# A WKV kernel on one Trainium2 core: a new hand-written order of all steps, with the first 21 loads on SyncE

## The chip, the cores and the metric

The kernel runs on one core of one Trainium2 chip. The metric is the device time of one execution in microseconds (us). A core has five engines that each work through a queue of their own, in order: TensorE (PE, with its weight loads PEld), VectorE (DVE), ScalarE (ACT), GpSimd (POOL) and SyncE (SP), which here only issues transfers. An instruction that has to wait holds up all that stands behind it in the queue of its engine. That holds for transfers too, since they are issued by instructions of POOL and SP.

## The reference

```python
# k, v: [16, 2048, 256] float32; w, u: [256]
for b in range(batch):
    aa, bb, pp = 0, 0, -1e38                      # per channel
    for t in range(seq_len):
        qq = maximum(pp, u + k[b, t])
        e1, e2 = exp(pp - qq), exp(u + k[b, t] - qq)
        output[b, t] = (e1 * aa + e2 * v[b, t]) / (e1 * bb + e2 + 1e-08)
        qq = maximum(pp - w + k[b, t], k[b, t])
        e1, e2 = exp(pp - w + k[b, t] - qq), exp(k[b, t] - qq)
        aa, bb, pp = e1 * aa + e2 * v[b, t], e1 * bb + e2, qq
```

It is a recurrence over time, apart for each batch and channel: a weighted mean of v, whose numerator `aa` and denominator `bb` are carried on with a running maximum `pp`.

## The kernel before, in words

The time axis is cut into 16 chunks of 128 steps, the 16 batches into four groups of four. A chunk of one group is a piece, n = 4 * chunk + group, so there are 64 pieces. A piece of k, of v and of the output is 512 KB each (`rows_of`, lines 126 to 128). The steps of a piece, by the short names that the order uses:

- `sk`, `k` load k, issued by SP or by POOL, into one of NK tiles `kr` (line 228). `sv`, `v` load v into one of NV tiles `vr` (line 238), and `CV` casts it on POOL to bf16 in one of NVB tiles `vb` (line 244). `vc` loads v with the cast in the transfer, into one of NVC tiles `vc` (line 241), and needs no `CV`; only POOL issues it. A load into a tile waits until the former piece in that tile has been read.
- `RK` rounds k on DVE into one of two tiles `km` (line 231).
- `LG` and `LGZ` make the logarithms of all weights on PE (lines 254 and 260). Pieces before H and from S on have two banks of half a piece each: `x` and `y` for even pieces, `d` and `n` for odd pieces before H. Between H and S there is one tile `X` of four banks in the place of `x` and `y`, and `d` and `n` are left to the sums below.
- `EXE` and `EX` take the exponential on ACT into the ring `ez` of 11 pieces: in halves (line 288, 1024 columns each), or in one instruction over `X` (line 286, 2048 columns).
- `TV` multiplies by v on DVE into the ring `ev` of 11 pieces (line 292).
- `DE` and `NU` make denominator and numerator on PE in 12 small matmuls each (line 306): sums over earlier steps, the step itself, and the row `RW` carried in from the chunks before.
- `LN` and `XP` turn the denominator into its inverse on ACT (lines 318 and 321) in one of NO output tiles `ot`, `MU` multiplies by the numerator on DVE (line 324), and `ST` stores with three transfers on SP (lines 328 and 330).

From the sums of a chunk's four pieces a chain of small steps makes the carry that the next pieces need, across four engines: `SU` (PE, line 360, reads `ez` and `ev` of four pieces), `CS` (DVE, 367), `TU` (PE, 372), `CT` (DVE, 377), `SL` (ACT, 380), `SH` (POOL, 385), `FR` (DVE, 390), `OF`, `OF2`, `OF3` (POOL, 395, 397, 399), `WE` (ACT, 402), `TBM`, `SCN`, `SPR` (DVE, 405, 410, 414), `TB` (PE, 426) and `RW` (DVE, 430). `KP` (POOL, 420 and 421) keeps the totals for the next chunk. `DE` and `NU` of chunk c wait for `RW` of c. Since `ez` holds 11 pieces, the exponentials of piece n wait for `DE` of piece n - 11 and for the `SU` that reads it.

`Z` and `Y` are matmuls with zeros (line 187) into a bank that is written over afterwards: they compute nothing and keep PE busy.

All of this stands in one list, `ORDER`, which is read from front to back; each word issues its instructions on their engines, so the list fixes the order in every queue. A letter d, n, x or y behind a word names the bank. Ahead of the list the program issues the loads of w and u on POOL, the first piece of k on SP, 13 zero matmuls (LEAD), and the constants, which POOL makes.

Of the kernel before, what the change touches and what calls it, by code (L numbers as in the profile page):

```python
# [21 lines left out]
H = 10  # L22
# [465 lines left out]
```

## Time and profile before

| | us |
|---|---|
| three runs | 290.6, 292.18, 294.44 |
| median | 292.18 |
| the profiled execution: its time | 294.63 |
| the profiled execution: its span, first to last instruction | 292.9 |
| busy in the span: PE, ACT, DVE, POOL | 253.2, 249.7, 244.7, 181.9 |

The profiled execution is 2.45 us above the median, and 1.73 us of its time lie outside its span. Times in the trace are counted from the start of the span. The profile page gives busy shares in 40 slices, groups of like instructions with the mean of one in ns, and the idle time ahead of them with what ended it. An answer by windows gives busy time for each engine in stretches that the reader chooses; the timeline gives single instructions in order, with their start, their duration and, in brackets, the idle time before them and what ended it. GB/s count a cast load by the bytes that it writes, half of those that it reads.

### The profile page before, as it was taken

The page shows a single profiled execution, that of the slowest core. Times are in us where ns is not written, and L with a number is a line of the kernel's source. Part 1 is how long each engine was busy: PE and PEld are TensorE (multiplying, and loading weights), DVE is VectorE, ACT ScalarE, POOL GpSimd, SP SyncE. Part 2 cuts the span into 40 slices and gives each one's busy share as a digit, 9 for nine tenths or more (in the row PEclk, how much of TensorE's full clock was granted, in tenths as well). Part 3 has the DMA queues.
Part 4 walks back from the last instruction along what each step waited for, and adds up shares of the span by engine and source line. Part 5 has one row for each costly group of instructions (what it writes and reads, how often), then busy time and mean ns, then how long its engine had stood idle before and what let it go on. Part 6 is the DMA issues. An engine that isn't in the chain of part 4 may idle for free. (4 is left out here: it accounts for less than half of the span.)

```text
span 292.9 us, 7115 instructions
## 1 busy us (share of the span) xinstructions
PE 253.2 (86%) x2775; PEld 132.8 (45%) x2775; DVE 244.7 (84%) x337; ACT 249.7 (85%) x243; POOL 181.9 (62%) x274
## 2 busy tenths in 40 slices
PE   8997988989889969989899999987988899898920
PEld 3444444545445434554445454544454455444410
DVE  4456669889889869999999999899999889898760
ACT  1774648989998888999999999999899999999960
POOL 7558968586777874668676958476657746432000
PEclk9998979999999999999999999999999999999995
DMA  7999997999999999999999999999999999995797
GB/s 227 348 348 329 358 189 247 329 385 286 373 346 294 383 359 398 357 313 289 373 352 344 403 288 352 391 313 296 386 333 309 352 317 364 310 273 158 226 265 215
DMA packets 70913, 93.54 MB, mean 319 GB/s; under 512 B 5204, under 2 KB 60000, under 8 KB 70880
## 3 DMA queue, kind: packets, MB, share of 16 engines
q0 software_dynamic: 27648, 52.19, 59.2%
q1 hardware_dynamic: 43232, 40.91, 45.4%
q8 instruction: 21, 0.34, 0.5%
q14 instruction: 12, 0.10, 0.1%
HBM read 67.12 MB, written 33.55 MB: 344 GB/s over the span
## 5 line engine op out<-in xcount | busy, mean ns | idle before, releaser
L286 ACT ACTIVATE ez<-X 128x2048 bf16<-128x2048 f32 x46 | 86.4, 1878 | 9.0 <-PE X L260 8.8
L324 DVE TENSOR_TENSOR ot<-n,ot 128x1024 f32<-128x1024 f32 x59 | 71.8, 1217 | 7.6 <-PE n L306 2.2
L321 ACT ACTIVATE ot<-ot 128x1024 f32<-128x1024 f32 x64 | 67.5, 1060 | 0.2
L318 ACT ACTIVATE ot<-d 128x1024 f32<-128x1024 f32 x58 | 59.6, 1027 | 2.4 <-PE d L306 1.9
L231 DVE CAST km<-kr 128x1024 fp32r<-128x1024 f32 x64 | 47.2, 743 | 11.5 <-DMA kr<-in_k_dram 9.4
L228 POOL DMA_DIRECT2D kr<-in_k_dram x56 | 44.2, 790 | 14.5 <-DVE km L231 9.4
L244 POOL CAST vb<-vr 128x1024 bf16<-128x1024 f32 x35 | 40.8, 1168 | 16.3 <-DMA vr<-in_v_dram 16.1
L292 DVE TENSOR_TENSOR ev<-ez,vb 128x2048 bf16<-128x2048 bf16 x35 | 45.0, 1288 | 2.7 <-POOL vb L244 2.7
L292 DVE TENSOR_TENSOR ev<-ez,vc 128x2048 bf16<-128x2048 bf16 x29 | 37.4, 1291 | 0.6 <-ACT ez L288 0.4
L260 PE MATMUL X<-km,NLE 128*128 128x512 f32 x92 | 33.7, 447 | 0.8 <-DVE km L231 0.8
L306 PE MATMUL n<-ev,LN 64*64 64x512 bf16 x236 | 24.0, 391 | 8.3 <-DVE ot L324 3.2
L254 PE MATMUL X<-WU,CO 1*128 1x512 f32 (+1 forms) x184 | 23.3, 495 | 6.4 <-ACT ez L286 5.6
L260 PE MATMUL X<-km,NLZ 128*128 128x512 f32 x92 | 28.8, 394 | 0.0
L306 PE MATMUL d<-ez,L 64*64 64x512 bf16 x232 | 23.7, 392 | 2.8 <-DVE RW L430 1.9
L238 POOL DMA_DIRECT2D vr<-in_v_dram x29 | 23.9, 823 | 2.5 <-DMA vc<-in_v_dram 1.5
L241 POOL DMA_DIRECT2D vc<-in_v_dram x29 | 23.2, 801 | 2.1 <-DVE TB L405 1.4
L306 PE MATMUL n<-RW,ROW 64*64 64x512 bf16 x236 | 23.5, 376 | 0.0
L306 PE MATMUL n<-ev,IdN 64*64 64x512 bf16 x236 | 23.5, 376 | 0.0
L306 PE MATMUL d<-RW,ROW 64*64 64x512 bf16 x232 | 23.2, 380 | 0.0
L306 PE MATMUL d<-ez,Id 64*64 64x512 bf16 x232 | 23.2, 380 | 0.0
L385 POOL TENSOR_TENSOR U<-U 128x64 f32<-128x64 f32 x16 | 9.5, 592 | 21.3 <-ACT U L380 21.2
L288 ACT ACTIVATE ez<-x 128x1024 bf16<-128x1024 f32 x13 | 13.3, 1025 | 10.7 <-PE x L254 5.4
(97 smaller groups left out, 431.6 us busy)
## 6 DMA issues: line engine op xcount, KB each, us to landing
kr<-in_k_dram POOLq DMA_DIRECT2D x56, 512.0 KB, 9.7
out_dram<-ot SPq DMA_DIRECT2D x64, 256.0 KB, 10.2
out_dram<-ot SPq DMA_DIRECT2D x128, 128.0 KB, 10.0
vr<-in_v_dram POOLq DMA_DIRECT2D x29, 512.0 KB, 9.6
vc<-in_v_dram POOLq DMA_DIRECT2D x29, 256.0 KB, 10.5
kr<-in_k_dram SPq DMA_DIRECT2D x8, 512.0 KB, 8.0
vr<-in_v_dram SPq DMA_DIRECT2D x6, 512.0 KB, 7.8
WU<-in_w_dram POOLq DMA_DIRECT2D x1, 8.0 KB, 5.3
```

Of the source, the lines that this page charges most:

```text
L228: K(q.dma_start(out=buf[n % len(buf)], in_=rows_of(x, n)))
L231: K(DVE.tensor_copy(KM[n % 2], KR[n % NK]))
L238: K(q.dma_start(out=VR[V_TILE[n] % NV], in_=rows_of(v, n)))
L244: K(POOL.tensor_copy(VB[V_TILE[n] % NVB], VR[V_TILE[n] % NV]))
L254: K(PE.matmul(log_tile(n, q)[:, i, :], CO[g:g + 1 + q, :], WU[g:g + 1 + q, :], start=q > 0 or n != FIRST, stop=q == 0 and n == FIRST, tile ...
L260: K(PE.matmul(log_tile(n, q)[:, i, :], (NLE, NLZ)[q], km[:, i, :], start=q == 0 and n == FIRST, stop=q > 0 or n != FIRST, skip_group_check ...
L286: K(SC.activation(t, BANKS["X"], ACT.Exp))
L292: K(DVE.tensor_mul(EV[n % REV], EZ[n % RING], vb.unsqueeze(1).broadcast_to([128, 2, 2, D])))
L306: K(PE.matmul(t[HS * x:HS * x + HS, i, :], left, right, start=j == 0, stop=m == "ROW", tile_position=(lo, HS * x), skip_group_check=True))
L318: K(SC.activation(OT[n % NO], AT.pop(("den", n)), ACT.Ln, scale=RS))
L321: K(SC.activation(OT[n % NO], OT[n % NO], ACT.Exp, scale=-1.0))
L324: K(DVE.tensor_mul(OT[n % NO], AT.pop(("num", n)), OT[n % NO]))
```

## The change

Seven loads go from POOL to SP: SP issues k.0 to k.12 and v.0 to v.7, 21 loads, where it issued k.0 to k.7 and v.0 to v.5. `v.7`, which was a load with cast, becomes a plain load with a `CV`; there are 28 loads with cast where there were 29. NK goes from 7 to 6 and NVC from 4 to 6 (a k tile has 4 KB in a partition, a `vc` tile 2 KB). H goes from 10 to 8: pieces 8 and 9 use the tile `X`. All other steps are the same in kind and number, but stand in a new order, and some of `SU`, `TU`, `TB`, `DE` and `NU` use another bank. There are 43 `Z` where there were 46, and 55 `Y` where there were 28. No function is changed.

The places that the prediction speaks of (the head of the list, its part behind the last exponential, and the words around it in between):

```diff
-NK = 7
+NK = 6
 NV = 3
-NVC = 4
+NVC = 6
...
-H = 10
+H = 8
...
 ORDER = """
-    sk.1 sv.0 sv.1 sk.2 sk.3 sv.2 sk.5 sk.4 RK.0 LG.0 RK.1 Z.1 Z.1 Z.1 Z.1 EXE.0 CV.0 LGZ.0 CV.1 LG.1 sv.3 EX.0 RK.2
-    sv.4 TV.0 Z.2 Z.2 Z.2 EXE.1 LGZ.1 LG.2 RK.3 EX.1 CV.2 LGZ.2 EXE.2 Z.3 Z.3 Z.3 Z.3 TV.1 sv.5 EX.2 LG.3 sk.6 sk.7
-    LGZ.3 EXE.3 RK.4 Z.4 Z.4 Z.4 Z.4 Z.4 Z.4 RK.5 EX.3 TV.2 LG.4 CV.3 Z.5 Z.5 EXE.4 LGZ.4 k.9 LG.5 TV.3 EX.4 k.8
-    LGZ.5 EXE.5 CV.4 Z.6 Z.6 Z.6 Z.6 Z.6 Z.6 EX.5 v.6 TV.4 vc.7 SU.0d RK.6 LG.6 CS.0 k.10 CV.5 TU.0d EXE.6 LGZ.6
-    CT.0 v.8 Z.7 Z.7 Z.7 Z.7 Z.7 Z.7 SL.0 EX.6 SH.0 RK.7 k.11 FR.0 LG.7 TV.5 k.12 Z.8 Z.8 Z.8 EXE.7 OF.0 RK.8 LGZ.7
-    OF2.0 LG.8 EX.7 RK.9 OF3.0 CV.6 Z.9 Z.9 EXE.8 LGZ.8 LG.9 TV.7 v.10 WE.0 EX.8 k.13 TBM.0 EXE.9 Z.10 Z.10 SCN.0
-    LGZ.9 vc.9 RK.10 EX.9 TV.6 LG.10 vc.11 vc.15 SPR.0 TB.0d EX.10 CV.8 SU.1n RW.0 KP.0 DE.0d CS.1 RK.11 TU.1n Z.11
-    Z.11 CV.10 CT.1 LG.11 SL.1 LN.0 RK.12 k.18 TV.10 NU.0n v.12 EX.11 DE.1d k.14 TV.9 LN.1 SH.1 Z.12 Z.12 k.15 TV.8
...
-    TV.61 Z.63 LG.63 WE.14 XP.52 MU.51 CV.62 LGZ.63 DE.53d EXE.63 TV.62 ST.51 NU.52n LN.53 MU.52 EX.63 Y.54 DE.54d
...
+    sk.1 sv.0 sv.1 sk.2 sk.3 sv.2 RK.0 Z.1 Z.1 Z.1 Z.1 Z.1 Z.1 RK.1 LG.0 LG.1 EXE.0 CV.0 LGZ.0 CV.1 sv.3 LGZ.1 EX.0
+    sk.4 RK.2 sk.6 EXE.1 Z.2 Z.2 Z.2 Z.2 sv.4 TV.0 sk.5 LG.2 EX.1 sk.8 RK.3 sk.7 TV.1 LGZ.2 EXE.2 Z.3 Z.3 Z.3 Z.3
+    Z.3 Z.3 EX.2 CV.2 LG.3 CV.3 sv.5 sk.9 LGZ.3 EXE.3 TV.2 Z.4 Z.4 Z.4 Z.4 Z.4 Z.4 EX.3 RK.4 LG.4 sk.10 TV.3 sv.6
+    EXE.4 CV.4 SU.0n LGZ.4 CS.0 EX.4 TU.0n CT.0 RK.5 Z.5 Z.5 Z.5 Z.5 SL.0 SH.0 sk.11 RK.6 LG.5 sv.7 FR.0 sk.12 OF.0
+    Z.6 EXE.5 LGZ.5 OF2.0 LG.6 RK.7 EX.5 CV.5 LGZ.6 EXE.6 Z.7 Z.7 OF3.0 RK.8 vc.9 LG.7 WE.0 EX.6 TBM.0 TV.4 LGZ.7
+    vc.11 EXE.7 Z.8 LG.8 SCN.0 EX.7 SPR.0 KP.0 EX.8 TB.0n CV.6 Y.0 Y.0 Y.0 RW.0 RK.9 v.10 DE.0d TV.5 LG.9 v.8 LN.0
+    k.13 RK.10 NU.0n TV.6 EX.9 k.14 Y.1 DE.1d CV.7 LN.1 LG.10 vc.13 TV.7 XP.0 k.15 RK.11 SU.1d EX.10 CS.1 TU.1d XP.1
+    LG.11 CV.10 RK.12 CT.1 MU.0 Y.2 Y.2 SL.1 EX.11 SH.1 v.12 FR.1 NU.1n ST.0 OF.1 DE.2d OF2.1 MU.1 OF3.1 LG.12 CV.8
+    WE.1 LN.2 ST.1 TV.10 k.16 Y.3 Y.3 Y.3 Y.3 Y.3 EX.12 v.14 TBM.1 RK.13 DE.3d SCN.1 XP.2 k.19 LG.13 TV.11 vc.15
...
+    NU.52n FR.14 LGZ.63 EXE.63 TV.61 Y.53 Y.53 Y.53 DE.53d EX.63 MU.52 OF.14 OF2.14 LN.53 OF3.14 DE.55x TV.63 ST.52
...
```

108 lines of the change are left out of this document (54 added, 54 removed).

## The prediction

> **What bounds the kernel now.** I read the page first: which engines are full, and when.
>
> ```profile
> span 292.9 us, 7115 instructions
> PE 253.2 (86%) x2775; PEld 132.8 (45%) x2775; DVE 244.7 (84%) x337; ACT 249.7 (85%) x243; POOL 181.9 (62%) x274
> ...
> ACT  1774648989998888999999999999899999999960
> ...
> DMA  7999997999999999999999999999999999995797
> ...
> HBM read 67.12 MB, written 33.55 MB: 344 GB/s over the span
> ```
>
> ACT, DVE and PE share the middle, all over nine tenths, with the DMA engines busy beside them. What is not full is the ramp (slices 1 to 8 of ACT) and the end. So I asked for windows over the ramp and the middle (the columns are busy us of PE, PEld, DVE, ACT and POOL, then granted clock, DMA share and GB/s).
>
> ```profile
> 24.00:32.00 8.00, 6.19 (x24) 3.17 (x24) 5.23 (x8) 2.84 (x4) 6.85 (x11) 0.79 1.10 335
> 32.00:38.00 6.00, 5.24 (x27) 2.42 (x25) 4.80 (x6) 5.60 (x7) 6.00 (x8) 1.00 1.03 346
> 38.00:50.00 12.00, 10.37 (x108) 5.21 (x108) 9.20 (x12) 6.97 (x7) 9.09 (x12) 0.86 0.91 188
> ...
> 85.00:113.00 28.00, 23.70 (x277) 12.48 (x270) 24.00 (x34) 23.61 (x22) 19.55 (x26) 1.00 1.13 349
> 113.00:229.00 116.00, 106.32 (x1245) 56.82 (x1245) 110.92 (x146) 111.91 (x103) 80.88 (x115) 1.00 1.11 343
> ```
>
> From 113 on ACT is busy 111.91 of 116. Before that two things show: ACT stands still for 5 of 12 us between 38 and 50, and there the transfers fall from 346 to 188 GB/s. The timelines of ACT, DVE, POOL and PE, one fence each, say why.
>
> ```profile
> 34.70 0.36 ACT L402 ACTIVATE G<-U 128x192 f32<-128x192 f32 x1
> 39.63 1.88 ACT L286 ACTIVATE ez<-X 128x2048 bf16<-128x2048 f32 x1 [1.51 <-PE X L260]
> 44.67 0.34 ACT L380 ACTIVATE U<-TS 128x128 f32<-128x128 f32 x1 [3.16 <-DVE TS L377]
> 46.29 1.88 ACT L286 ACTIVATE ez<-X 128x2048 bf16<-128x2048 f32 x1 [0.36 <-PE X L260]
> 51.89 1.87 ACT L286 ACTIVATE ez<-X 128x2048 bf16<-128x2048 f32 x1
> 55.49 1.88 ACT L286 ACTIVATE ez<-X 128x2048 bf16<-128x2048 f32 x1 [0.31 <-PE X L260]
> 113.12 1.88 ACT L286 ACTIVATE ez<-X 128x2048 bf16<-128x2048 f32 x1 [0.52 <-PE X L260]
> 227.87 1.88 ACT L286 ACTIVATE ez<-X 128x2048 bf16<-128x2048 f32 x1
> ```
>
> ```profile
> 6.41 0.70 DVE L231 CAST km<-kr 128x1024 fp32r<-128x1024 f32 x1 [0.34 <-DMA kr<-in_k_dram]
> 11.12 0.69 DVE L231 CAST km<-kr 128x1024 fp32r<-128x1024 f32 x1 [4.01 <-DMA kr<-in_k_dram]
> 17.14 1.30 DVE L231 CAST km<-kr 128x1024 fp32r<-128x1024 f32 x2 [2.46 <-DMA kr<-in_k_dram]
> 25.68 0.41 DVE L367 COPY ts<-d 128x256 f32<-128x256 f32 x1
> 40.84 0.69 DVE L430 CAST RW<-d 128x512 bf16<-128x512 f32 x1 [1.04 <-PE d L426]
> ```
>
> ```profile
> 31.24 0.44 POOL L399 TENSOR_SCALAR U<-U 128x64 f32<-128x64 f32 x1
> 43.61 0.76 POOL L228 DMA_DIRECT2D kr<-in_k_dram  x1 [2.89 <-DVE km L231]
> ```
>
> ```profile
> 42.09 0.64 PE L306 MATMUL d<-ez,L 64*64 64x512 bf16 x4
> ```
>
> The eight ACT rows are `WE.0`, the exponentials of piece 10, `SL.1`, and pieces 11, 12, 13, 26 and 55. `RW.0` comes at 40.84, so `DE.0` at 42.09. Piece 11 reuses the `ez` tile of piece 0 and must wait for it: 6.66 us lie between pieces 10 and 11. In the same time POOL stands at `k.18`, whose tile is free only after `RK.11` (43.61), with v.12, k.14 and k.15 queued behind it: that is the hole in the transfers. From piece 13 to 26 a piece takes 57.63 / 13 = 4.43 us, from 26 to 55 it takes 114.75 / 29 = 3.96 us. So the bound is a late first carry in the ramp, a stretch that runs behind, then a full ACT (with DVE close to it).
>
> **The change, part by part.** (1) Loads on SP. The three DVE waits above are for the 2nd, 5th and 9th load of SP: 6.41, 11.12, 17.14, or 1.5 us a load. I take load number i (from 0) to land at 5.1 + 1.5 i. In the new row k.4 is still the 9th (17.1), k.6 comes at 18.6, v.4 20.1, k.5 21.6, k.8 23.1, k.7 24.6, v.5 26.1, k.9 27.6, v.6 30.6, v.7 33.6, k.12 35.1. The k come earlier, v.6 and v.7 later. SP issues in order and now waits at `sv.3` for `CV.0`, with thirteen loads behind it, `sk.4` first. `CV.0` and `CV.1` run here:
>
> ```profile
> 8.86 2.02 POOL L244 CAST vb<-vr 128x1024 bf16<-128x1024 f32 x2
> ...
> 14.14 1.45 POOL L244 CAST vb<-vr 128x1024 bf16<-128x1024 f32 x1 [3.25 <-DMA vr<-in_v_dram]
> ```
>
> so SP goes on at about 9.9, while loads already issued land until 14.1 (the second row, for v.2): no hole, 0 us. POOL gives up seven issues and takes one more cast:
>
> ```profile
> L228 POOL DMA_DIRECT2D kr<-in_k_dram x56 | 44.2, 790 | 14.5 <-DVE km L231 9.4 <-DVE TB L405 2.6 <-DVE U L390 1.9
> L244 POOL CAST vb<-vr 128x1024 bf16<-128x1024 f32 x35 | 40.8, 1168 | 16.3 <-DMA vr<-in_v_dram 16.1
> ```
>
> 7 x 0.79 - 1.17 = 4.4 us less, all of it ahead of 36 us, where POOL was full (6.00 of 6.00) and the first carry passed through it.
>
> (2) The first carry. Each step is put after the last one it waits for, with durations from the rows. `TV.3` needs `CV.3` (v.3 at 15.6) and `EX.3`, which slips to some 17.7 behind six zero matmuls, and `RK.4`: it ends at 19.9. `SU.0` 20.0 to 21.2; `CS.0` 21.2 (it was 25.68, queued behind `RK.6`, whose k.6 was the 13th load); `SL.0` 22.9; `SH.0`, `FR.0` (behind `RK.5` and `RK.6`) until 24.5; `OF.0`, `OF2.0` until 25.6; then POOL has `CV.5` ahead of `OF3.0` and waits for v.5: 26.1 + 1.17, `OF3.0` ends at 27.7 (it was 31.68); `WE.0` 27.8 (34.70); `SCN.0` behind `TV.4` 29.6; `TB.0` behind `LG.8` 31.3; `RW.0` 31.7 (40.84); `DE.0` 32.5 (42.09). The carry comes 9 us earlier.
>
> (3) Pieces 8 to 13, with H = 8. A piece over `X` needs 1.9 us on PE and then 1.88 on ACT, one after the other. The LN and XP that the early carry sets free fill ACT meanwhile. `EX.8` 31.5, `EX.9` 35.5, `EX.10` 39.2 (it was 39.63); `EX.11` waits for nothing of the ring now, only for PE behind `TU.1`: 43.3 (46.29); `EX.12` 47.0 (51.89); `EX.13` 50.8 (55.49). That is 4.7 us. `LN.3` is done by then, which it was not before: one more instruction off the rest.
>
> ```profile
> L318 ACT ACTIVATE ot<-d 128x1024 f32<-128x1024 f32 x58 | 59.6, 1027 | 2.4 <-PE d L306 1.9 <-DMA out_dram<-ot 0.2
> L187 PE MATMUL d<-Z 128*128 128x512 bf16 x46 | 14.5, 409 | 0.5 <-ACT ot L318 0.5
> L286 ACT ACTIVATE ez<-X 128x2048 bf16<-128x2048 f32 x46 | 86.4, 1878 | 9.0 <-PE X L260 8.8
> ```
>
> 1.0 us, so -5.7 in all. Bounds: 0, if a late v.10 eats it (rival C), and 9, the whole advance of the carry.
>
> (4) Pieces 13 to 26. The pace was 4.43 against 3.96 later. If the new order has no hole behind it, up to 13 x 0.47 = 6.1 us more go. If the transfers are as late as before, nothing. I take 0, nearer to the trace: loads on POOL are again queued behind casts and behind tiles not yet free (`CV.10`, `k.19`).
>
> (5) Zero matmuls. 24 more, at most 24 x 14.5 / 46 = 7.6 us of PE. PE is idle for 40 us of the span and they stand ahead of waits: 0. Where that cover is gone (six ahead of `LG.3` and of `LG.4`) they are counted in (2). Bounds -1 (less of the low clock, 0.79 and 0.86 above) and +2.
>
> (6) Two pieces more over `X`: 1.88 for two of 1.02, which is -0.2 each on ACT; but its idle ahead of such a piece is 9.0 / 46 = 0.2. Sum 0. Six tiles for k and other banks for the small sums: 0, bounds below (rival D).
>
> (7) The end.
>
> ```profile
> 282.99 1.23 DVE L324 TENSOR_TENSOR ot<-y,ot 128x1024 f32<-128x1024 f32 x1 [0.79 <-DMA out_dram<-ot]
> ```
>
> ```profile
> 286.31 0.54 SPq L328 DMA_DIRECT2D out_dram<-ot  x1
> ...
> 288.24 0.55 SPq L328 DMA_DIRECT2D out_dram<-ot  x1
> 288.84 1.26 SPq L330 DMA_DIRECT2D out_dram<-ot  x2
> ```
>
> SP issues one store each 1.93 us and is behind the last `MU` by three of them. Twelve stores stand behind the last exponential in both lists, so this stays; one more LN stands there in the new list (`LN.53`): +0.9. Bounds -1 and +2.
>
> Sum: -5.7 + 0 + 0 + 0 + 0.9 = -4.8. The profiled execution (294.63, which is 292.9 and 1.73 around it) would become 289.8. It lies 2.45 above the median of the runs, 292.18; from that, 287.4.
>
> **The rivals.** A is the sum: 287.4, or 284 to 291 by its bounds in (5), (6) and (7) and half of those in (3).
>
> B, the stretch goes too: no hole at 38 to 50, so pieces 13 to 26 run at 3.96. 287.4 - 6.1 = 281.3. For it: in the later stretch 29 pieces of 1.57 MB (k, v and output, 512 KB each) took 114.75 us, 397 GB/s, so the transfers can follow. Against it: 85 to 113 showed 349 GB/s at a share of 1.13 without keeping up, so B gets half the chance of A. The Trainium skill (DMA: Bandwidth & Descriptors, Specifications) gives about 358 GB/s of HBM for a core; by that figure 100.67 MB take an estimated 281 us without ramp or end, and B could not be. The trace's 397 GB/s over 114.75 us do not agree with it.
>
> C, the hole only moves: POOL has `CV.10` ahead of `SH.1`, `v.12` and `OF.1`, and v.10 is issued only after `CV.6`, at about 33. I took it to land in 6.5 us. The view of line 238 gives this for loads into `vr`:
>
> ```profile
> DMA to landing us min/median/max: 5.9/9.5/14.5
> ```
>
> At 14.5 it lands at 47.5, `CV.10` ends near 48.7, and `SH.1` is 7 us late. `RW.1`, which I place at 52, comes at 59 and `DE.4` at 60, when `EX.15`, due near 58.5 (50.8 and two pieces), stands waiting for the `ez` tile: 1.5 us. What was issued before (eight loads on POOL behind 35.1, at 1.5 each) has landed by 47, so the transfers stand for some 3 us until `v.12` and those behind it flow. 287.4 + 4.5 = 291.9. By this the change does not do what it says: the work moves and the time stays.
>
> D, slower: six k tiles starve `RK`. Two rows bear on it, the casts of k and the landing of k's loads.
>
> ```profile
> L231 DVE CAST km<-kr 128x1024 fp32r<-128x1024 f32 x64 | 47.2, 743 | 11.5 <-DMA kr<-in_k_dram 9.4 <-PE n L260 2.1
> ```
>
> ```profile
> kr<-in_k_dram POOLq DMA_DIRECT2D x56, 512.0 KB, 9.7
> ```
>
> With seven a tile can be away for 7 x 3.96 = 27.7 us, with six for 23.8. Of that landing takes 9.7 us in the median, and waits of POOL for a free tile come on top (9.4 us in all, line 228 above). If the pace of 4.43 then lasts to piece 55, it costs 29 x 0.47 = 13.6: 301.0. It decides once more than ten pieces behind the 26th run at that pace (10 x 0.47 = 4.7), and is slower by 2% after 23. Against it: with seven tiles DVE waited 9.4 us for k in all, and 6.8 of them are the three waits before 18.
>
> **How the numbers follow.** Chances: A 0.45, B 0.22, C 0.20, D 0.13. The time is that of A, 287.4. A measurement of this kernel can tell about 2% from no change, so the bounds are 286.3 and 298.0. Below 286.3 lie B and about a third of A: 0.22 + 0.15 = 0.37. Above 298.0 lies most of D: 0.10. Between them: 0.53. The range leaves out the lower half of B and the upper part of D: 280.0 to 296.0; A's own is 284 to 291.
>
> **What the changed profile would show.** Right: `RW.0` (line 430, first) near 32 and the first `DE` near 32.5; no stretch under 300 GB/s between 15 and 60; the fifth exponential over `X`, counting piece 8 as the first, starting at 47, the sixth at 51; POOL's first wait for a free k tile under 1 us. (4) is read from the spacing of line 286 up to its 19th instance (piece 26): 4.43 for A, 3.96 for B. C shows as a wait of POOL for a `vr` load of over 5 us ahead of line 385's second instance. D shows as DVE waits for `kr` all through 113 to 229. The forecast is wrong if `WE.0` still stands after 33, or if the pace behind piece 26 is over 4.1.

## The result and the profile after

The changed kernel is not faster: over 20 runs each, its median is 294.03 us (292.99 to 296.68) against 293.08 (290.6 to 299.75) for the kernel before, a ratio of 1.0054 with a 95% interval of 1.003 to 1.0079. The forecast was 4.8 us less; what came is about 1 us more by the medians and 1.6 by the ratio. The profiled execution took 293.75 us, with a span of 292.0. Every ratio here is made of the undisturbed runs alone, so it need not be the quotient of two medians, and of the four kernels whose profiles were taken in disturbed executions (`e5_ramp_of3`, `e7_old_sp`, `e8_new_to_30`, `e9_old_to_30`) only the timed runs are used.

First the page of the changed kernel: totals, and the slices of ACT, of the granted clock and of the transfers.

```profile
span 292.0 us, 7159 instructions
PE 259.7 (89%) x2799; PEld 133.3 (46%) x2799; DVE 243.6 (83%) x337; ACT 250.6 (86%) x241; POOL 171.4 (59%) x268
...
ACT  1754688978899999989999999999979999999970
...
PEclk9999599999999999999999999999999999999995
DMA  7999998999999999999999999999999999974887
GB/s 224 348 348 351 299 332 246 321 365 329 274 364 341 396 312 345 301 388 400 384 297 399 369 257 392 345 345 393 295 371 319 345 399 307 307 225 111 255 237 214
...
L232 DVE CAST km<-kr 128x1024 fp32r<-128x1024 f32 x64 | 49.9, 784 | 6.5 <-DMA kr<-in_k_dram 6.0
```

Little moved in the totals. ACT has 250.6 us of work where it had 249.7, and PE 259.7 where it had 253.2, part of which is matmuls at a low clock: the fifth slice of PEclk is a 5. In the slices of ACT the sixth, 36.5 to 43.8 us, is an 8 where it was a 4; but the ninth to eleventh are 7, 8, 8 where they were 8, 9, 9, and the 18th is an 8 where it was a 9. The 13th to 16th, 88 to 117 us, are 9s where they were 8s; that stretch is taken up again below. The windows say how much (busy us of PE, PEld, DVE, ACT and POOL, then granted clock, DMA share, GB/s).

```profile
32.00:38.00 6.00, 6.00 (x30) 2.78 (x30) 3.81 (x5) 2.99 (x3) 5.54 (x7) 0.58 1.25 293
38.00:50.00 12.00, 11.20 (x116) 5.55 (x116) 8.59 (x12) 10.30 (x10) 7.04 (x12) 1.00 0.94 273
85.00:113.00 28.00, 26.42 (x304) 13.91 (x306) 24.86 (x37) 26.71 (x25) 18.63 (x30) 1.00 1.13 344
113.00:229.00 116.00, 107.56 (x1243) 56.45 (x1236) 109.43 (x143) 110.46 (x101) 80.43 (x114) 1.00 1.12 353
```

From 38 to 50 ACT works 10.30 us of 12 (6.97 before), and the transfers run at 273 GB/s (188 before): the hole that the prediction was built on is mostly gone. In its place 32 to 38 has 2.99 us of ACT (5.60 before), 293 GB/s (346 before) and a granted clock of 0.58 (1.00 before). From 32 to 50 together ACT has won 0.72 us, not the 3.33 of 38 to 50 alone. From 113 to 229 ACT does 110.46 us where it did 111.91. Now the single instructions of the ramp, one fence each for ACT, POOL, DVE and PE. (One line was added in the source, so line 286 of before is 287 here.)

```profile
28.98 0.37 ACT L403 ACTIVATE G<-U 128x192 f32<-128x192 f32 x1 [2.76 <-POOL U L400]
29.25 1.00 ACT L289 ACTIVATE ez<-y 128x1024 bf16<-128x1024 f32 x1
...
33.73 1.88 ACT L287 ACTIVATE ez<-X 128x2048 bf16<-128x2048 f32 x1 [1.64 <-PE X L261]
...
38.49 1.88 ACT L287 ACTIVATE ez<-X 128x2048 bf16<-128x2048 f32 x1 [0.63 <-PE X L261]
...
42.24 1.87 ACT L287 ACTIVATE ez<-X 128x2048 bf16<-128x2048 f32 x1
...
45.95 1.88 ACT L287 ACTIVATE ez<-X 128x2048 bf16<-128x2048 f32 x1 [0.66 <-PE X L261]
...
49.54 1.88 ACT L287 ACTIVATE ez<-X 128x2048 bf16<-128x2048 f32 x1 [0.55 <-PE X L261]
...
53.17 1.88 ACT L287 ACTIVATE ez<-X 128x2048 bf16<-128x2048 f32 x1
```

```profile
27.38 1.04 POOL L245 CAST vb<-vr 128x1024 bf16<-128x1024 f32 x1 [3.24 <-DMA vr<-in_v_dram]
28.51 0.44 POOL L400 TENSOR_SCALAR U<-U 128x64 f32<-128x64 f32 x1
...
40.73 1.10 POOL L245 CAST vb<-vr 128x1024 bf16<-128x1024 f32 x1 [1.18 <-DMA vr<-in_v_dram]
...
45.37 0.30 POOL L386 TENSOR_TENSOR U<-U 128x64 f32<-128x64 f32 x1 [3.54 <-ACT U L381]
...
51.07 0.75 POOL L229 DMA_DIRECT2D kr<-in_k_dram  x1 [0.81 <-DVE km L232]
```

```profile
34.19 0.69 DVE L431 CAST RW<-n 128x512 bf16<-128x512 f32 x1 [2.50 <-PE n L427]
```

```profile
30.31 0.59 PE L188 MATMUL X<-Z 128*128 128x512 bf16 x1 [2.73 <-ACT ez L289]
...
35.29 0.64 PE L307 MATMUL d<-ez,L 64*64 64x512 bf16 x4
...
39.48 0.41 PE L307 MATMUL d<-ez,L 64*64 64x512 bf16 x4
```

This is one chain. POOL waits 3.24 us for v.5 ahead of `CV.5` (27.38), `OF3.0` stands behind that cast (28.51), and `WE.0` behind `OF3.0`: ACT stands still for 2.76 us (28.98). `EX.6` stands behind `WE.0` on ACT, so it starts at 29.25; PE wants to write the tile that `EX.6` reads and waits 2.73 us (30.31); it had been idle since 27.58, so what `EX.6` reads was long there. After that wait PE has the clock of 0.58, its `DE` matmuls take 0.64 (35.29) where the same ones take 0.41 later (39.48), and the first carry `RW.0` comes at 34.19, `DE.0` at 35.29. Before they came at 40.84 and 42.09, so the carry is 6.7 us earlier, not 9. The exponentials of pieces 8 to 13 (the rows from 33.73 to 53.17) came 2.2 to 3.0 us behind the forecast, piece 13 at 53.17 for 50.8.

### The profile page after: what moved, and what is told of

Same layout as the page of the kernel before. It is cut to its first block, busy times and chain, and to the rows that moved or that the text cites. A ratio compares the mean times of both kernels' runs of the same rounds, so it can differ in the third digit from the quotient of the medians.

```text
span 292.0 us, 7159 instructions
## 1 busy us (share of the span) xinstructions
PE 259.7 (89%) x2799; PEld 133.3 (46%) x2799; DVE 243.6 (83%) x337; ACT 250.6 (86%) x241; POOL 171.4 (59%) x268
## 4 chain that ended last, share of the span: by engine, by line
PE 33%; DMA 30%; ACT 16%; DVE 9%; issue 3%; POOL 3%; SPq 3%; DVEq 0%; ACTq 0%; POOLq 0%
DMA out_dram<-ot 24%; PE X L261 10%; ACT ez L287 8%; DMA vr<-in_v_dram 6%; PE d L307 5%; PE n L307 4%; PE X L255 4%; DVE ot L325 4%; ACT ot L319 3%; ACT ot L322 3%; PE n L361 2%; PE d L188 2%; DVE km L232 2%; DVE ev L293 2%; POOL vb L245 1%
## 5 line engine op out<-in xcount | busy, mean ns | idle before, releaser
L287 ACT ACTIVATE ez<-X 128x2048 bf16<-128x2048 f32 x48 | 90.1, 1876 | 11.8 <-PE X L261 11.3
L232 DVE CAST km<-kr 128x1024 fp32r<-128x1024 f32 x64 | 49.9, 784 | 6.5 <-DMA kr<-in_k_dram 6.0
L229 POOL DMA_DIRECT2D kr<-in_k_dram x51 | 40.1, 787 | 17.4 <-DVE km L232 11.8
L261 PE MATMUL X<-km,NLE 128*128 128x512 f32 x96 | 35.6, 453 | 0.0
L293 DVE TENSOR_TENSOR ev<-ez,vc 128x2048 bf16<-128x2048 bf16 x28 | 34.3, 1225 | 0.0
L261 PE MATMUL X<-km,NLZ 128*128 128x512 f32 x96 | 30.5, 399 | 0.0
L255 PE MATMUL X<-WU,CO 1*128 1x512 f32 x192 | 24.7, 504 | 5.1 <-ACT ez L287 4.5
L239 POOL DMA_DIRECT2D vr<-in_v_dram x28 | 22.5, 805 | 1.7 <-POOL vb L245 0.6
L386 POOL TENSOR_TENSOR U<-U 128x64 f32<-128x64 f32 x16 | 6.1, 384 | 27.2 <-ACT U L381 27.0
L255 PEld LDWEIGHTS X<-WU,CO 1*128 1x128 f32 x192 | 9.4, 185 | 27.6 <-ACT ez L287 17.6
```

What stands on the lines that cost most here:

```text
L229: K(q.dma_start(out=buf[n % len(buf)], in_=rows_of(x, n)))
L232: K(DVE.tensor_copy(KM[n % 2], KR[n % NK]))
L239: K(q.dma_start(out=VR[V_TILE[n] % NV], in_=rows_of(v, n)))
L255: K(PE.matmul(log_tile(n, q)[:, i, :], CO[g:g + 1 + q, :], WU[g:g + 1 + q, :], start=q > 0 or n != FIRST, stop=q == 0 and n == FIRST, tile ...
L261: K(PE.matmul(log_tile(n, q)[:, i, :], (NLE, NLZ)[q], km[:, i, :], start=q == 0 and n == FIRST, stop=q > 0 or n != FIRST, skip_group_check ...
L287: K(SC.activation(t, BANKS["X"], ACT.Exp))
```

## The experiments

The theory after the result was: the new ramp is a gain, smaller than forecast, and the order of the words behind it loses more than that gain. Its rivals: the ramp itself is no gain; a bound common to both kernels (the transfers) takes back whatever the ramp wins; the new tile counts starve the loads. For each kernel the median, and the ratio to the kernel before with its 95% interval, are given. All kernels compute the whole output; only zero matmuls, which compute nothing, are added or removed in some.

**The ramp alone, the rest alone.** `e1_new_ramp` follows the new list up to `EX.15` and the old one behind, with the old tile counts.

```diff
-NK = 7  NVC = 4  H = 10
+NK = 7  NVC = 4  H = 8
-(words of the old list up to EX.15)
+(words of the new list up to EX.15)
 ... LG.16 LN.6 TV.15 XP.5 RK.17 (and all that follows in the old list)
```

> New order up to the exponential of piece 15, then the old order for all that is left, with the old tile counts (NK 7, NVC 4) and H = 8. In the profiles piece 15 starts at 63.1 in the new kernel and at 65.7 in the old, so the new ramp is 2.6 us ahead here. Theory M (the new ramp is real, and the new order's own middle gives it back): the old rest keeps the lead, 293.1 - 2.6 = 290.5, ratio 0.991. Rival K (the middle catches up with whatever starts early, since both orders meet the same bound there): 293.1, ratio 1.000, with the lead gone by piece 30 as in the new kernel, where it is -0.1. Rival R (the ramp itself costs something that the profile after hides): over 1.003.

`e2_old_ramp` is the reverse: old list up to `EX.15`, new one behind, with six tiles for k and for `vc`; k.19 and some words at the seam are moved for that.

```diff
-NK = 7  NVC = 4
+NK = 6  NVC = 6
-... SU.2d k.19 EX.12 RK.13 NU.1n
+... SU.2d EX.12 RK.13 k.19 NU.1n
-(words of the old list behind EX.15)
+(words of the new list behind EX.15)
```

> The opposite: old order up to the exponential of piece 15, then the new order for the rest, with the new tile counts (NK 6, NVC 6) and H = 10; one load (k.19) moved behind the cast that frees its tile. Theory M: the middle of the new order is worse by what it gave back, so 294.0 + 2.6 = 296.6, ratio 1.012. Rival K: 293 to 294, ratio 1.000 to 1.003. The two runs together: if ramp and rest add up, the ratios of the two multiply to that of the new kernel, 1.005.

Measured: 291.63, ratio 0.997 (0.9934 to 1.0005), and 295.43, ratio 1.0084 (1.0049 to 1.0119). The two ratios multiply to 1.0054, which is the whole change. Of 293 us these are some 0.9 us won by the ramp, which is not clear of nothing, and some 2.5 lost by the order behind it.

**Where behind it.** `e8_new_to_30` follows the new list up to `EX.30` (k.43, k.47 and k.60 moved, since six tiles for k stay), `e9_old_to_30` the old list up to there.

```diff
 NK = 6  NVC = 6  H = 8
 (words of the new list up to EX.30)
-(words of the new list behind it)
+(words of the old list behind it)
```

> New order to the exponential of piece 30, old order behind it, new tile counts (NK 6, NVC 6), H = 8; three k loads (43, 47, 60) moved behind the cast that frees their tile. In the profiles the new order's lead goes from 2.6 at piece 15 to 0.1 at piece 30, while e1 holds 4.1 and 5.2. Theory P (the loss lies in the new order of pieces 16 to 30): as the new kernel, ratio 1.003 to 1.006, with a lead of under 1.5 us at piece 30. Rival Q (the loss lies behind piece 30, at the end of the new order or in its tile counts): as e1, 0.997.

```diff
 NK = 7  NVC = 4  H = 10
 (words of the old list up to EX.30)
-(words of the old list behind it)
+(words of the new list behind it)
```

> The opposite cut: old order to the exponential of piece 30, new order behind it, old tile counts, H = 10. Theory P: 293.0, ratio 0.999 to 1.002, since the new order behind piece 30 is no worse. Rival Q: ratio 1.008 as in e2, where the new order began at piece 16.

Measured: `e8` 294.15, ratio 1.0053 (1.0012 to 1.0094), the same as the full change: behind piece 30 the new order neither wins nor loses, as far as an interval of 0.4% to each side can tell. `e1` and `e8` have the new ramp in common and differ in pieces 16 to 30 and the tile counts; their intervals do not overlap, though by little. `e9` came to 301.18, ratio 1.0282 (1.0221 to 1.0342), a miss, which I put down to the old tile counts under the new order. `e3_old_tiles` tries these counts on the whole new list:

```diff
-NK = 6  NVC = 6
+NK = 7  NVC = 4
-... CS.3 vc.27 RK.19 ... TV.19 k.23 ... Z.28 vc.35 NU.16n ... TV.27 ST.16
+... CS.3 RK.19 ... TV.19 vc.27 k.23 ... Z.28 NU.16n ... TV.27 vc.35 ST.16
```

> The new order with seven k tiles and four tiles for cast loads, as before; two cast loads (27 and 35) moved behind the multiply that frees their tile. Theory M and K: 294.0, ratio 1.003 to 1.006, since waits for k in the middle are short in the profile after (6.0 us in all). Rival D of the prediction (six k tiles cost time): faster than the new kernel by over 1 us, ratio 1.000 or below.

Measured 300.73, ratio 1.0238 (1.0185 to 1.0291), slower than any theory expected: the new order needs the new counts, not the old ones. In its groups POOL waits 4.3 us for `TV` to free a `vc` tile, where the changed kernel's loads into `vc` wait 0.3 in all. So `e9` was repeated with the new counts:

```diff
-NK = 7  NVC = 4
+NK = 6  NVC = 6
-... SPR.3 k.28 XP.10 LG.21 MU.9 CV.22 LN.11 RK.22 v.26
+... SPR.3 XP.10 LG.21 MU.9 CV.22 LN.11 RK.22 k.28 v.26
 (k.19, k.31, k.33 and k.35 moved likewise)
```

> e9_old_to_30 again, but with the new tile counts (NK 6, NVC 6); five k loads (19, 28, 31, 33, 35) moved behind the cast that frees their tile. e9 and e3 both ran the new order with four tiles for cast loads and came out at 1.024 to 1.028, so e9 could not tell where the new order loses. Theory P (the loss lies in pieces 16 to 30 of the new order): 0.998 to 1.002. Rival Q (it lies behind piece 30): 1.006 to 1.010. If it is still over 1.02, the tile counts were not the cause in e9.

Measured 297.02, ratio 1.0148 (1.0079 to 1.0218). That missed too, though it is well under the 1.0282 of `e9`, so the counts were a part of that loss. In its trace some 3 us go at pieces 30 to 34, right where the lists are joined (18.93 us from the one exponential to the other, 15.30 in the changed kernel), so it says nothing on the list behind the seam. That nothing is lost there rests on `e8` alone. But the part ahead of the seam bears on the counts: it is the old order with the new counts, and ACT has done 88.43 us in it by 113 (39.77 by 60, then 23.02 and 25.64), where the kernel before had done 85.04 and, in the second profile shown next, 87.87. So the new counts by themselves lose nothing there, and by that what parts `e8` from `e1` is the order of pieces 16 to 30.

**A second look at the kernel before.** The forecast rested on one profiled execution, so the same kernel was profiled again.

> The kernel before, unchanged, for a second profile: its first one was 1.55 us above its median. If single executions differ by where the granted clock falls, this profile shows other places under 1.00 than 24 to 32 and 38 to 50, and a span of 290 to 292. If not, the same places and 292 to 293.

It took 291.72, with a span of 290.0. Its clock is 1.00 from 24 to 32, where the first had 0.79, and 0.86 from 38 to 50, as in the first. The windows of four executions side by side: the kernel before in its first profile (85 to 113 stands in the prediction) and in its second, the changed kernel (85 to 113 stands above), and `e1`. The fourth figure, ACT's busy time, is the one to compare.

```profile
0.00:60.00 60.00, 53.83 (x380) 26.27 (x381) 39.11 (x67) 38.21 (x39) 43.54 (x78) 0.94 1.01 299
60.00:85.00 25.00, 22.38 (x259) 12.04 (x262) 22.28 (x29) 23.22 (x22) 18.96 (x26) 1.00 1.13 347
...
113.00:130.00 17.00, 15.87 (x195) 8.51 (x194) 16.71 (x24) 16.70 (x15) 10.37 (x17) 1.00 1.05 363
```

```profile
0.00:60.00 60.00, 54.23 (x392) 26.46 (x396) 40.86 (x67) 38.65 (x39) 43.69 (x80) 0.94 1.03 305
60.00:85.00 25.00, 22.47 (x279) 12.26 (x267) 23.69 (x31) 23.22 (x23) 19.92 (x27) 1.00 1.13 344
85.00:113.00 28.00, 25.85 (x288) 13.46 (x278) 25.00 (x33) 26.00 (x24) 19.66 (x27) 1.00 1.12 352
113.00:130.00 17.00, 15.57 (x191) 8.47 (x193) 16.65 (x23) 16.81 (x16) 11.47 (x19) 1.00 1.11 359
```

```profile
0.00:60.00 60.00, 54.16 (x406) 26.16 (x410) 38.40 (x66) 39.80 (x38) 38.34 (x72) 0.94 1.04 311
60.00:85.00 25.00, 22.69 (x233) 11.45 (x225) 23.22 (x29) 21.05 (x21) 18.19 (x27) 1.00 1.13 326
...
113.00:130.00 17.00, 15.65 (x185) 7.60 (x177) 14.42 (x20) 15.18 (x14) 10.44 (x15) 1.00 1.12 352
```

```profile
0.00:60.00 60.00, 53.94 (x420) 26.12 (x420) 40.45 (x67) 41.27 (x39) 39.49 (x74) 0.97 1.05 320
60.00:85.00 25.00, 22.84 (x275) 12.07 (x275) 23.21 (x35) 21.92 (x22) 21.00 (x29) 1.00 1.14 344
85.00:113.00 28.00, 25.87 (x278) 13.19 (x274) 25.77 (x33) 25.99 (x24) 19.88 (x27) 1.00 1.11 357
113.00:130.00 17.00, 15.47 (x176) 8.65 (x177) 16.76 (x23) 16.84 (x18) 12.22 (x19) 1.00 1.11 344
130.00:229.00 99.00, 90.83 (x1014) 47.81 (x1012) 90.75 (x121) 91.36 (x85) 66.59 (x95) 0.95 1.11 345
```

ACT has nearly the same work in all of them (249.7 and 250.6 us on the pages of before and of the changed kernel), so what it has done by 130 us is the lead of a kernel. The first profile of before stands at 101.74 (38.21 + 23.22 + 23.61 + 16.70), the second at 104.68, the changed kernel at 102.74, `e1` at 106.02. Against the second profile the changed kernel is 1.94 behind, and its span is 2.0 longer; against the first it is 1.00 ahead, and its span is 0.9 shorter. Both times the lead at 130 is, within 0.1 us, the difference of the spans, so all of it is made before 130. And it is made so, against the second profile: the changed kernel wins 1.15 by 60 (39.80 against 38.65), loses 2.17 from 60 to 85, wins 0.71 to 113, and loses 1.63 from 113 to 130. Against the first it is 1.59 won, 2.17 lost, 3.10 won and 1.52 lost. The figure by 60 moves from execution to execution: `e3` and `e15`, with the same list up to there, have 39.81 and 38.59. The windows from 60 to 130 together separate the two orders in every profile used:

| ACT busy, us of 70 between 60 and 130 | |
|---|---|
| new order there: changed kernel, `e2`, `e3`, `e4`, `e14`, `e15`, `e16` | 62.94, 62.89, 61.58, 62.90, 61.66, 62.55, 62.63 |
| old order there: before, before again, `e1`, `e6`, `e10`, `e13` | 63.53, 66.03, 64.75, 64.26, 65.87, 64.22 |

(The figures are those of the fences and of the same windows of the other kernels; in `e11` the lists are joined inside the stretch.) The gap between the two rows, 0.59 at its least, is smaller than the 2.50 between two profiles of one kernel. The last window, 113 to 130, parts them better: 13.80 to 15.33 with the new order, 16.21 to 16.84 with the old. The stretch from 85 to 113 of the first profile, 23.61 of 28, which the forecast took for a property of the kernel, is 26.00 in the second and 24.89 in `e13`, with the same order there: most of it belonged to that execution.

**What the new ramp is made of.** Three kernels take one part each. `e13_old_h8` is the kernel before with H = 8 alone.

```diff
-H = 10
+H = 8
-... OF3.0 CV.6 Z.9 Z.9 EXE.8 LGZ.8 LG.9 TV.7 v.10 WE.0 EX.8 k.13 TBM.0 EXE.9 Z.10 Z.10 SCN.0 LGZ.9 vc.9 RK.10 EX.9 TV.6
+... OF3.0 CV.6 EX.8 Z.9 Z.9 LG.9 TV.7 v.10 WE.0 k.13 TBM.0 EX.9 Z.10 Z.10 SCN.0 vc.9 RK.10 TV.6
```

> The old kernel with H = 8 alone: pieces 8 and 9 go over the tile X in one exponential each, with the exponential where its first half stood; nothing else is moved. Theory: two instructions of 1.88 us for four of 1.02 save 0.2 us each on ACT, but X cannot be filled while it is read, so pieces 9 and 10 come later by about 1 us; the ramp waits for the carry (SL.1 at 44.7) all the same: 1.000, give or take 0.003. Rival: pieces 9 to 11 lose 2 us or more that stay to the end, 1.007.

Measured 298.28, ratio 1.021 (1.0153 to 1.0267), more than either theory expected. Its window shows the old hole made deeper: 100 GB/s from 38 to 50 where the kernel before had 188.

```profile
38.00:50.00 12.00, 10.03 (x89) 5.33 (x92) 5.72 (x9) 5.73 (x5) 5.35 (x9) 0.69 0.63 100
```

My reading, not tried further: one tile in the place of two half pieces makes PE and ACT wait for each other, and with a late carry nothing fills the time. `e7_old_sp` is the kernel before with six loads moved from POOL to SP, and `e6_pool_loads` is `e1` with seven moved back.

```diff
-... k.9 LG.5 TV.3 EX.4 k.8 ... v.6 ... k.10 CV.5 ... k.11 FR.0 ... k.12
+... sk.9 LG.5 TV.3 EX.4 sk.8 ... sv.6 ... sk.10 CV.5 ... sk.11 FR.0 ... sk.12
```

> The old kernel with k.8 to k.12 and v.6 issued by SP, at the same places of the old list; nothing else is changed. Theory S2 (SP as issuer is worth something by itself): the loads no longer stand behind POOL's casts, piece 9 to 11 start up to 1 us earlier, 292, ratio 0.997. Rival O2 (it is worth something only with an order that asks for k first): 1.000, with the hole in the transfers between 38 and 50 still there, since k.18 still stands ahead of k.14 on POOL.

```diff
-... sk.8 RK.3 ... sk.9 ... sk.10 TV.3 sv.6 ... sk.11 RK.6 LG.5 sv.7 FR.0 sk.12
+... k.8 RK.3 ... k.9 ... k.10 TV.3 v.6 ... k.11 RK.6 LG.5 v.7 FR.0 k.12
```

> e1_new_ramp with k.8 to k.12, v.6 and v.7 issued by POOL again, at the same places of the list. It tells what SyncE as the issuer is worth. Theory S (the loads on SP carry the new ramp): POOL issues each only when it gets there, behind casts that wait for v; about the 2 to 5 us that the ramp leads are lost, ratio 1.003 to 1.010. Rival O (the order alone carries it): as e1, 0.997, give or take 0.003.

Measured: 292.3, ratio 0.9937 (0.9892 to 0.9982), and 300.07, ratio 1.0213 (1.014 to 1.0287), against 0.997 for `e1`. The move is worth 0.6% by itself and 2.4% inside the new ramp: on POOL the loads stand behind the casts, and the carry behind both. In `e6` `WE.0` comes 5.87 us later than in `e1` (28.89), after a wait for POOL that is longer by 3.27 (2.77 in `e1`), as this row of ACT shows:

```profile
34.76 0.37 ACT L401 ACTIVATE G<-U 128x192 f32<-128x192 f32 x1 [6.04 <-POOL U L398]
```

**One word.** The first carry waits at `CV.5`; so `OF3.0` is put ahead of it, in the changed kernel (`e4`) and in `e1` (`e5`).

```diff
-... EX.5 CV.5 LGZ.6 EXE.6 Z.7 Z.7 OF3.0 RK.8
+... EX.5 OF3.0 CV.5 LGZ.6 EXE.6 Z.7 Z.7 RK.8
```

> The new kernel with one word moved: the last offset step of chunk 0 (OF3.0) goes ahead of the cast of v.5 on POOL, which waits 3.2 us for its load. In the profile after ACT stands 2.8 us at the weights of chunk 0 (line 403) behind it, PE then 2.7 us at the bank of piece 8, and the granted clock falls to 0.58 between 32 and 38. Expected of the ramp by all theories: the weights near 25 instead of 29, the first carry (line 431) near 31 instead of 34.2, no low clock. Theory M: the gain of about 2.5 us is kept only as far as the middle lets it; if nothing catches up, 291.5, ratio 0.995. Rival K: 294.0, ratio 1.003, whatever the ramp does.

> e1_new_ramp (new order to the exponential of piece 15, old order behind it, old tile counts) with OF3.0 ahead of CV.5, as in e4_of3_first. Theory M, as e1 (0.997) and e2 (1.0084) left it: what the ramp saves is kept by the old rest. In the profile of e4 pieces 6 to 9 start 2.9 to 5.3 us before those of the profile after, but only 0.5 us of that is left at piece 13, so the gain over e1 is small: 291.0, ratio 0.993 to 0.997. If the carry itself were worth its advance to the end, 288.5, ratio 0.985. Rival K: 293, ratio 1.000.

Measured: `e4` 292.91, ratio 0.9991 (0.9957 to 1.0025), below the interval of the changed kernel; `e5` 290.95, ratio 0.9906 (0.986 to 0.9952). In `e4` the first carry is 3.9 us earlier than in the changed kernel, as this row of DVE shows:

```profile
30.29 0.69 DVE L431 CAST RW<-n 128x512 bf16<-128x512 f32 x1 [0.64 <-PE n L427]
```

ACT does 40.44 us by 60 then, 0.64 more, and from 60 to 130 it does 62.90, as in the changed kernel. No low clock was expected in the ramp; it is 1.00 from 32 to 38 now, but 0.72 from 38 to 50, where ACT does 6.24 us. The chain read above is confirmed. Its part, 0.63% by the two ratios, is smaller than the 0.84% that `e2` puts on the order behind the ramp.

**The instruction behind the loss.** In 60 to 85 and 113 to 130 PE waits ahead of `TU.3` and `TU.6`, with the logarithms `LG.18` and `LG.30` behind it, and zero matmuls stand around. Three kernels try that: `e14` takes 11 zero matmuls out, `e15` puts `LG.18` ahead of `TU.3`, `e16` has both and `e4`.

```diff
-... CV.14 Z.15 Z.15 LG.15 ... LN.8 Z.19 Z.19 Z.19 MU.7 ... ST.15 Z.28 vc.35 ... SPR.5 Z.29 MU.17 ... LN.20 Z.30 Z.30 Z.30 Z.30 k.36
+... CV.14 LG.15 ... LN.8 MU.7 ... ST.15 vc.35 ... SPR.5 MU.17 ... LN.20 k.36
```

> The new kernel without the 11 zero matmuls of pieces 15 to 30 (Z.15, Z.19, Z.28, Z.29, Z.30). They write zeros into X and so wait for the exponential before; behind Z.30 on PE stands TU.6, and CT.6 waits 1.6 us for it (line 378) in the profile after. Theory Z (zero matmuls ahead of real work cost the stretch 113 to 130, where ACT is busy 15.18 us in the new kernel, 14.95 in e2 and 16.70 in the old): 1 to 1.5 us less, ratio 1.001, ACT near 16.5 in that stretch. Rival Y (they keep the clock up): the granted clock falls below 1.00 somewhere between 60 and 130, ratio 1.010.

```diff
-... RK.19 TU.3d XP.6 SPR.2 NU.6n CT.3 vc.19 TB.2d SL.3 LG.18 XP.7
+... RK.19 LG.18 TU.3d XP.6 SPR.2 NU.6n CT.3 vc.19 TB.2d SL.3 XP.7
```

> The new kernel with one word moved: the logarithms of piece 18 (LG.18) go ahead of TU.3 on PE. In the profile after PE waits 1.15 us for CS.3 at TU.3 (line 373), and LG.18 and with it the exponential of piece 18 stand behind it; ACT is busy 21.05 us of 25 between 60 and 85 there, 21.24 in e2, 23.22 in the old kernel. Theory T (that queue is what the stretch loses): ACT near 22.5 in it, 1 to 1.5 us less in the end, ratio 1.001. Rival U (the carry of chunk 2, which shares bank d behind TU.3, comes later instead and takes it back): 1.005.

> The new kernel with the three edits of e4, e14 and e15 together. If the theory is right that the new order loses at these three places and not at a common bound, the gains add: 1.8 us (e4 against the new kernel) and 1 to 1.5 each, ratio 0.990 to 0.993. If the places only trade with others, as in rival K, 0.999 like e4 alone.

Measured: `e14` 296.36, ratio 1.0157 (1.0094 to 1.022); `e15` 295.27, ratio 1.0105 (1.0047 to 1.0163); `e16` 292.62, ratio 1.0012 (0.9971 to 1.0053), no better than `e4`. Both theories fell. Without the zero matmuls the granted clock is 0.93 from 60 to 85 where it was 1.00. But `e16` lacks the same 11, keeps 1.00 there, and is not clear of `e4` in time. So what they are worth changes with the words around them. The two windows, `e14` first:

```profile
60.00:85.00 25.00, 21.77 (x224) 10.66 (x216) 22.01 (x28) 19.94 (x19) 18.18 (x26) 0.93 1.12 325
```

```profile
60.00:85.00 25.00, 21.73 (x244) 11.67 (x248) 23.38 (x29) 21.23 (x22) 17.37 (x26) 1.00 1.08 293
```

With `LG.18` early ACT still has only 20.54 us there. What ACT waits for can be read: from 60 to 85 five exponentials of the changed kernel wait 3.06 us for PE to fill `X`, where two wait 1.04 us in the second profile of before. What makes PE late with `X` stays open; shown is only the stretch and that the loss goes with the new order.

**A version better than both.** `e1` has a stretch of its own in which ACT falls back: 91.36 us from 130 to 229, where before did 95.11 to 95.21. It is a half clock, in 200 to 210:

```profile
195.00:200.00 5.00, 3.50 (x35) 2.00 (x27) 4.98 (x5) 5.00 (x5) 4.49 (x6) 0.91 1.24 277
200.00:205.00 5.00, 5.00 (x34) 2.40 (x34) 3.77 (x6) 1.76 (x3) 1.62 (x3) 0.50 1.10 369
205.00:210.00 5.00, 5.00 (x34) 2.05 (x33) 3.50 (x4) 3.08 (x3) 3.52 (x5) 0.57 1.06 380
```

ACT is busy 1.76 and 3.08 of 5 us there, so 5.16 us idle. What stands ahead of it are two short waits of PE, and the same two stand in the kernel before, 5 us later, with the clock at 1.00. First PE in `e1`, then PE in the kernel before, then that kernel's window.

```profile
198.30 0.40 PE L426 MATMUL d<-Id,CB 128*128 128x128 bf16 x4 [0.76 <-DVE CB L414]
...
199.43 1.17 PE L372 MATMUL n<-Sel,ts 128*128 128x96 f32 x4 [0.74 <-DVE ot L324]
```

```profile
203.29 0.40 PE L426 MATMUL d<-Id,CB 128*128 128x128 bf16 x4 [0.76 <-DVE CB L414]
...
204.43 0.69 PE L372 MATMUL n<-Sel,ts 128*128 128x96 f32 x4 [0.74 <-DVE ot L324]
```

```profile
200.00:205.00 5.00, 3.50 (x36) 1.98 (x28) 4.97 (x5) 5.00 (x5) 4.49 (x6) 1.00 1.24 290
```

`e10_warm` is `e5` with four zero matmuls in the first of those waits.

```diff
-... LN.39 k.53 XP.38 TB.10d k.54
+... LN.39 k.53 XP.38 Y.39 Y.39 Y.39 Y.39 TB.10d k.54
```

> e5_ramp_of3 with four zero matmuls more, put ahead of the turn back of chunk 10 (TB.10), where PE stands 0.76 and then 0.73 us in the profile of e5. There the granted clock falls to 0.57 between 200 and 205 and pieces 48 to 52 lose 2.7 us of a lead of 4.6. Theory W (the half clock is what takes that lead, in most executions): 2 to 3 us less than e5, 288.5, ratio 0.982, and a lead of 4.5 us held up to piece 63. Rival V (the fall comes only in some executions, or comes elsewhere instead): as e5, 0.99, give or take 0.004.

Measured 288.79 (287.91 to 290.67), ratio 0.9861 (0.9802 to 0.992): faster than the kernel before and than the changed one. Its granted clock there:

```profile
200.00:205.00 5.00, 4.52 (x44) 2.50 (x44) 5.00 (x7) 3.78 (x4) 3.60 (x6) 1.00 1.05 402
```

Whether the four matmuls alone are a gain over `e5` the times do not settle, for the two intervals overlap; the clock of 1.00 and ACT's 94.88 us from 130 to 229 are one profile. Its clock is 1.00 by 60 as well, where `e4` and `e16` have 0.94 and 40.44 us of ACT with nearly the same ramp; the four matmuls stand far behind, so that is this execution's luck. But ACT is at 108.07 us by 130 in it, 3.39 more than before's second profile, and its span is 3.2 shorter: a lead won in the ramp and kept is worth its full size at the end. That rules out a common bound behind the ramp, at least down to this time.

## Why the prediction was wrong, by its steps

(1) Loads on SP. The estimate of v.5 was 26.1; its cast could begin at 27.38. No hole opened at `sv.3`: the second to fourth slices of the page have 348, 348 and 351 GB/s. Right in kind; worth 0.6% alone, and a condition of the ramp (`e6`).

(2) The first carry. `WE.0` at 28.98 for 27.8, `RW.0` at 34.19 for 31.7, `DE.0` at 35.29 for 32.5. Two things were not in the chain: that `EX.6` and `EX.7` stand behind `WE.0` on ACT, so that a late `WE.0` stops PE as well; and that PE then runs at 0.58. I took PE's durations as given. With `OF3.0` one place ahead, `RW.0` comes at 30.29: the 31.7 was within reach.

(3) Pieces 8 to 13. The step gave -4.7 to piece 13 and -5.7 in work of ACT. Piece 13 came 2.3 earlier (53.17 for 55.49), and ACT had done 1.59 us more by 60 (39.80 against 38.21), 1.15 against the second profile. So this step failed by its size: the hole at 38 to 50 closed, as the mechanism said, but most of what ACT won there it lost from 32 to 38, by the late and slow carry of step (2). The term was about twice too large for the exponentials and four to five times for ACT's work, and in time the ramp alone (`e1`) is worth some 0.9 us. In microseconds this is the larger of the two misses. With that mended and the clock at 1.00, `e10` has 42.20 by 60, 3.99 more than the first profile and 3.55 more than the second.

(4) Pieces 13 to 26, "I take 0". This is the step that failed and turned the sign: by `e2` the order behind the ramp costs some 2.5 us, more than the ramp wins. It asked only whether the transfers of the new order would be late, and bounded the answer by a gain of 6.1 and by zero; it gave no row for a loss, though all words were rearranged there. Against the second profile the stretch 60 to 85 loses 2.17 us and 113 to 130 loses 1.63, and the latter lies behind piece 26, where the prediction counted nothing. The base was off as well. Piece 13 to piece 26 takes 55.57 us in the changed kernel (to 108.74), 4.27 a piece and not the 4.43 of the first profile; but the second profile of before has 54.90 there, 4.22 a piece. So 2.7 of the 6.1 us that rival B could win were one execution's own, and what the new order seemed to win in that stretch was not its own. The pace does not compare like work either: 25 LN and XP stand between the two exponentials in the new list and 27 in the old, which is about 2 us of ACT. From piece 26 to 55 the changed kernel takes 4.07 a piece, 118.12 us, where before took 114.75, with 59 and 58 of them. Of that difference 1.9 us lie between pieces 27 and 28, 5.76 us where before took 3.87; one LN more stands there, about 1 us. The exponentials of pieces 26, 27 and 28:

```profile
108.74 1.88 ACT L287 ACTIVATE ez<-X 128x2048 bf16<-128x2048 f32 x1
...
112.41 1.87 ACT L287 ACTIVATE ez<-X 128x2048 bf16<-128x2048 f32 x1
...
118.17 1.88 ACT L287 ACTIVATE ez<-X 128x2048 bf16<-128x2048 f32 x1 [0.26 <-PE X L261]
```

(5) Zero matmuls, 0: no run tries the added ones as a whole. Taking 11 away makes the changed kernel slower (1.0157 against 1.0054, intervals apart), but not when two other words are moved as well (`e16`, 1.0012, beside `e4`, 0.9991).

(6) Two more pieces over `X`, 0: in the old order H = 8 costs 2.1%, so if it pays, then only with an early carry; within the new ramp it was not tried apart. Six tiles for k: right, DVE waits 6.0 us for k in all (line 232) where it waited 9.4.

(7) The end: +0.9 was forecast, no loss shows. From 229 to 262 ACT does 31.73 us, 31.87 in the second profile of before, and the spans differ by what the lead at 130 says.

The rivals. B did not come: from 113 to 229 ACT is at 110.46, behind before's 111.91. C, the hole only moves, by `CV.10` and `SH.1`: the time is nearest to its 291.9, but not by its mechanism. `CV.10` waited for v.10 for 1.18 us (40.73), not for over 5, and `SH.1` waited at 45.37 for ACT, 3.54 us, not for POOL. Against D stand the 6.0 us above, and `e3`, which is slower with the seven tiles (and four for `vc`); POOL's first wait for a free k tile is 0.81 us (51.07), as the forecast said for the case that D does not hold. That no stretch would be under 300 GB/s between 15 and 60 was wrong in two windows, 293 and 273. Of the two signs that were named for being wrong neither came: `WE.0` stood at 28.98 and not after 33, and the pace behind piece 26 was 4.07, just under 4.1. So the forecast could fail without either of them.

Against a common bound of the transfers at the time of the kernel before stands `e10`, which ends 3.2 us sooner than the second profile of that kernel. The 397 GB/s of the prediction counts pieces; by the transfers that landed in those 114.75 us (29 of k, 27 of v, the stores of 27 pieces) it is 379. The Trainium skill (DMA: Bandwidth & Descriptors, Specifications) gives a core about 358 GB/s of HBM. The 379, and the 363 of `e10` from 85 to 113, lie above it; the 100.67 MB over the whole span of `e10`, 286.8 us, are 351 GB/s, so no run here shows that the whole kernel can be faster than the 281 us estimated from that figure.

## What to carry to other kernels

Judge a rearranged list by one engine's cumulative busy time at a few marks, in two or more profiles of the kernel before: a slow stretch in one profile can be that execution's own. When all words behind a change are rearranged too, zero is not a neutral estimate for them; join the two lists at a mark and time both halves. Walk a carry's chain through each queue for what stands behind its waiting instruction, not only for what it waits for.

## What the runs showed of the hardware

The granted clock of PE can fall after a stretch in which PE was by no means idle. In `e1` it was 0.50 and 0.57 from 200 to 210, and PE had been busy 3.50 of the 5 us ahead, with no wait over 0.76 us; in the kernel before, the same work with the same waits kept 1.00. The changed kernel has 0.58 at 32 to 38 after a wait of 2.73 us, `e1` after nearly the same wait, 2.71 us, has 0.73 in that window, and `e4` has its fall, to 0.72, from 38 to 50 instead. The Trainium skill (TensorE: Matmul & The Clock Gate, What's actually happening) says that the gate looks at activity in a free-running window of about 3.4 us; that the same sequence falls at one start and not at another agrees with a window that does not follow the kernel, and its cold state, half the clock, with the 0.50. Its rule of no gaps over about 3.4 us (HAM oscillation) does not suffice here: no gap of `e1` in the 5 us ahead was over 0.76 us. The fall in `e1` left ACT idle for 5.16 us, and ACT did 3.75 less from 130 to 229 than in before's second profile (91.36 against 95.11).

Runs of one kernel go with their clock: those of `e10` at a mean granted clock of 0.985 to 0.988 took 287.91 to 288.95 us, those at 0.972 and 0.973 took 290.67 and 290.2.
